# Hybrid stick-breaking and sparse attention: value products in one burst a unit later, low-part score pairs first and together

## The chip, the cores and the metric

One core of one Trainium2 chip. The metric is the device time of one launch in microseconds (us); lower is better. TensorE is called PE, VectorE DVE, ScalarE ACT, GpSimd POOL and SyncE SP; PEld is TensorE's weight load.

## The reference

Two decoder layers on 512 tokens of width 1024. In each layer two token mixers run on the same normalised input `h`, and their gated outputs are merged:

```python
proj = h @ w_in                      # 1024 x 5912, split into all the parts below
# (A) stick-breaking attention, 8 heads of 64, causal
z = q @ k.T * scale
w = where(mask, exp(log_sigmoid(z) + between), 0)   # between: reversed cumulative sum of log_sigmoid(-z)
o_a = w @ v
# (B) native sparse attention, 8 query heads, 2 key heads of 64
p_cmp = softmax(q @ kc.T)            # 31 compressed blocks
o_s = softmax(q @ k_slc.T) @ v_slc   # selected blocks: all 8 of 8, so causal attention
o_w = softmax(q @ k_win.T) @ v_win   # window of 512: causal attention too
o_b = g0 * o_cmp + g1 * o_s + g2 * o_w
merged = sigmoid(ga) * ((o_a * silu(z_a)) @ w_up_a) + sigmoid(gb) * ((o_b * silu(z_b)) @ w_up_b)
x = x + merged @ w_out
```

## The kernel before

Everything is float32. A product that must be exact is made from two halves: `hi` holds the operand rounded to the format that PE streams fast, `lo` the rest, and three products (hi by hi, hi by lo, lo by hi) are added up in one PSUM bank. PSUM's eight banks have fixed roles: `acc` (2), `S` (4, scores), `o` (1, output of the value products), `tp` (1, transposes and small things).

A layer has three stages.

- **X**: stick-breaking attention, 16 steps (four pairs of heads by four key blocks, `sb_qk`, `sb_cs`, `sb_pv`), with the projections for both attentions put between the steps.
- **Y**: sparse attention in 16 units, four query groups `j` by four query blocks `i`; unit `(j, i)` has `i + 1` key blocks. `nsa_qk` makes the scores of the two key heads for the selected and the window branch, takes the row maximum (DVE), the exponentials (ACT) and scales the rows by gate over sum (DVE) into `pr`. `nsa_pv` transposes `pr` by PE through `tp`, one key block (four 128x128 transposes) at a time, has ACT (even blocks) or DVE (odd blocks) copy the bank to `pT`, and multiplies by the values into `o` (four products for a key block in the source, eight instructions in the trace, two passes each). Between all this stand the products of the gate projections. `cmp_qk`, `cmp_t` and `cmp_pv` do the compressed branch once for each `j`.
- **Out**: the last three gate projections, the two up-projections and the output projection.

PE's order is written out by hand. A `Pacer` keeps a clock of its own (`mm` and `tr` add an estimate for each product), and `pump(us)` takes products from a queue of projections (`fill`) until that clock has moved on by so much. `Y_FILL` holds 21 projections of 24 products for stage Y; when they are used up, `pump` returns at once. In unit `u` stage Y pumps until `Y_LAT` (8 to 10 us) after the scores of that unit, emits the scores of unit `u + 1`, and then the transposes and value products of unit `u`. The other engines' orders come from a scheduler.

PE is used in three shapes. Most products and the transposes use the full 128 by 128 array. The value products have 64 output columns; those of the two key heads use the two column halves, side by side. The low-part score products have 64 contracted rows (`sK2` in stage X, `kN2` in stage Y); those of two heads use the two row halves, side by side, into two banks. The value products of both attentions are called column-split here, the low-part score pairs row-split.

Of the kernel before, what the change touches and what calls it, by code (L numbers as in the profile page):

```python
# [13 lines left out]
F32 = mybir.dt.float32  # L14
# [3 lines left out]
AF = mybir.ActivationFunctionType  # L18
# [4 lines left out]
P = 128  # L23
# [27 lines left out]
def kernel(  # L51
# [238 lines left out]

    def new_h():
        hs = H()
        hs.hh, hs.hl = [], []
        hs.ssq = cp.tile([P, S], F32, tag="ssq", name="ssq")
        return hs
# [46 lines left out]
    def mm(out, lhsT, rhs, start, stop, us, **kw):  # L342
        T.matmul(out, lhsT, rhs, start=start, stop=stop, **kw)  # L343
        pc.tick(us)
# [176 lines left out]
    def g_tile(tag, dt=F32, n=S):  # L521
        return gp.tile([P, n], dt, tag=tag, name=tag, bufs=dict(G_TAGS)[tag])
# [110 lines left out]
    for l in range(depth):  # L633
        yt = [None] * 4
        last = l == depth - 1
        with ExitStack() as lc:
# [111 lines left out]
            def mlp_w2(ht, hv2):  # L748
                with tc.high_priority(offset=PRIO_SB):
# [3 lines left out]
                    for t in range(2):  # L753
                        mm(pt[:, HD:P], hv2[:, t].rearrange("p a c -> p (a c)"), w2t[:, 1, t], False, t == 1, 0.2,
                           skip_group_check=True)
# [121 lines left out]
            def sb_qk(t):  # L877
# [5 lines left out]
                for h, z in enumerate(zb):  # L883
                    mm(z[:, :n], R.sK1[:, h, ks], R.sX[:, h, kb * P:], True, False, n * .00043)
                for h, z in enumerate(zb):
                    gs = slice(h * HD, (h + 1) * HD)
                    mm(z[:, :n], R.sK2[gs, ks], R.sX[gs, h, kb * P:], False, True, n * .00043)
                with tc.high_priority(offset=PRIO_SB):
# [105 lines left out]
            def nsa_qk(j, i):  # L994
# [10 lines left out]
                for hf, (a, b) in enumerate(halves):  # L1005
                    w = (b - a) * 256
                    for g in range(2):
                        mm(sb[g][hf][:, :w], nX[:, g, qs], kN1[g][:, a:b].rearrange("p k t c -> p (k t c)"),
                           True, False, w * .00043)
                    for g in range(2):  # L1010
                        gs = slice(g * HD, (g + 1) * HD)
                        mm(sb[g][hf][:, :w], nX[gs, g, qs], kN2[gs, a:b].rearrange("p k t c -> p (k t c)"),
                           False, b < nk, w * .00043)
                for g in range(2):
# [20 lines left out]

            def nsa_pv(o, pr, i, gap):
                nk = i + 1
                qs = slice(i * P, (i + 1) * P)
                pend = None

                def pv(kb, pT):
                    for t in range(2):
                        for g in range(2):
                            mm(o[g * HD:(g + 1) * HD, qs], vN[:, kb, t * P + g * HD:t * P + (g + 1) * HD],
                               pT[:, g, t], False, kb == nk - 1 and t == 1, 0.115, skip_group_check=True)

                for kb in range(nk):
                    pt = t_bank()
                    ptv = pt.rearrange("p (g t q) -> p g t q", g=2, t=2)
                    for g in range(2):  # L1050
                        for t in range(2):
                            tr(ptv[:, g, t], pr[g][:, kb, t], identf)
                    pT = py.tile([P, 2, 2, P], F32, tag="pT", name="pT", bufs=3)
                    with tc.high_priority(offset=PRIO_SB):
                        if kb % 2 == 0:
                            A.activation(pT.rearrange("p g t q -> p (g t q)"), pt, AF.Copy)  # L1056
                        else:
                            V.tensor_copy(pT.rearrange("p g t q -> p (g t q)"), pt)
                    if pend is not None:
                        pv(*pend)  # L1060
                    pend = (kb, pT)
                    pc.pump(gap)
                pv(*pend)

# [86 lines left out]
            with ExitStack() as ly:  # L1151
# [4 lines left out]
                ready = pc.now + Y_LAT[0]  # L1156
                for u in range(16):
                    j, i = u // NT, u % NT
                    pc.pump(ready - pc.now)
                    if u == 0:  # L1160
                        pcT = cmp_t(sc)
                    if u < 15:
# [4 lines left out]
                        if i == 2 and j < 2:  # L1167
                            set_nX(j + 2, n_q[j + 2])
                    if i == 0:
                        o = cmp_pv(pcT)  # L1170
                    nsa_pv(o, pr.pop(u), i, Y_GAP)
                    if i == 2 and j < 3:
                        pc.until(lambda: j + 1 in n_in)
                        sc = cmp_qk(j + 1)
                    if i == 3:
                        if ("z", j) in done:
                            V.scalar_tensor_tensor(yt[j][:, 1], o, 0.5, yt[j][:, 1], op0=ALU.mult, op1=ALU.mult)
                        else:
                            A.activation(yt[j][:, 1], o, AF.Copy)
                        done.add(("o", j))  # L1180
                        if j < 3:
                            pcT = cmp_t(sc)
                pc.drain()

        eng.copy = A.copy
        with ExitStack() as lc:
# [44 lines left out]
            if not last:  # L1231
                hs2 = new_h()
            for n in range(KD):
# [59 lines left out]
```

## Time and profile before

| | us |
|---|---|
| three timed runs | 1053.28, 1056.89, 1058.15 |
| their median | 1056.89 |
| the profiled execution: span on the core | 1055.7 |
| PE busy | 1015.3 (96%) |
| DVE busy | 754.2 (71%) |
| ACT busy | 443.2 (42%) |
| POOL busy | 253.8 (24%) |

The profile gives a span for its execution, from the first to the last instruction, and no time around it; the span lies between the timed runs, 1.2 us under their median. The chain of work that ended last is PE by 66%, DVE by 14%. Since matmuls are pipelined, what one costs is read from the distance of its start to the next one's start, not from its own duration. In the first layer stage X runs to about 224 us, stage Y to 426 us and the rest to 546 us; in the second layer the same stages end at about 738 us, 941 us and the end.

### The profile page before, as it was taken

Reading aid. Unit: us, or ns where it says so; the run is one execution under the profiler, and the core shown is the slowest. Engines: PE = TensorE matmul, PEld = TensorE weight load, DVE = VectorE, ACT = ScalarE, POOL = GpSimd, SP = SyncE. Lnnn points to the kernel's source line nnn. Section 1 sums busy time; section 2 is a strip of 40 time slices with the busy share of each in tenths; the row PEclk is TensorE's granted clock in tenths of the full one; section 3 lists DMA queues with packets and bytes.
Section 4 is the critical chain, followed back from the end, with each engine's and each line's share of the span. In section 5 each row is a group of like instructions: output and inputs, shape, how many; then the busy total and the mean of one; then the engine's idle time right before and its main releaser. Section 6 shows DMA issues by size and latency. Waiting matters only on the chain.

```text
span 1055.7 us, 14761 instructions
## 1 busy us (share of the span) xinstructions
PE 1015.3 (96%) x5379; PEld 775.3 (73%) x5379; DVE 754.2 (71%) x1468; ACT 443.2 (42%) x1070; POOL 253.8 (24%) x288
## 2 busy tenths in 40 slices
PE   7999899899999999999999989989999999999998
PEld 5876666677777777888887657757777777778886
DVE  7889878968777766575576987787886866665641
ACT  4453446654333332633333534565443323336221
POOL 4173454541111101000014525636201110100000
PEclk9999999999999999999999989989999999999999
DMA  8422334312221222244632223350312221224331
GB/s 280 118 61 61 85 100 109 76 41 65 56 61 41 61 61 60 80 122 121 177 105 71 65 69 99 85 124 20 80 49 53 60 61 40 62 60 140 96 107 57
DMA packets 161769, 88.05 MB, mean 83 GB/s; under 512 B 38417, under 2 KB 157473, under 8 KB 161697
## 3 DMA queue, kind: packets, MB, share of 16 engines
q1 hardware_dynamic: 160816, 84.99, 29.9%
q0 software_dynamic: 704, 2.11, 0.5%
q8 instruction: 42, 0.69, 0.3%
q14 instruction: 31, 0.25, 0.1%
q10 hardware_dynamic: 176, 0.03, 0.0%
HBM read 80.81 MB, written 6.29 MB: 83 GB/s over the span
## 4 chain that ended last, share of the span: by engine, by line
PE 66%; DVE 14%; issue 9%; POOL 6%; ACT 4%; DMA 2%; POOLq 0%; SPq 0%; ACTq 0%; DVEq 0%
PE acc L343 40%; PE S L343 14%; PE o L343 6%; PE tp L347 4%; DVE wlo L402 2%; POOL whi L160 1%; DVE f_t L683 1%; ACT y L490 1%; PE tp L343 1%; POOL sum L931 1%; ACT e L217 1%; DVE y L493 1%; DVE e L896 1%; POOL sum L930 1%; DMA raw<-in_w_in_dram 1%
## 5 line engine op out<-in xcount | busy, mean ns | idle before, releaser
L343 PE MATMUL acc<-hl,whi 128*128 128x512 f32 x640 | 259.7, 406 | 1.6 <-DVE hl L586 1.4
L343 PE MATMUL acc<-hh,whi 128*128 128x512 f32 x640 | 259.9, 406 | 1.0 <-DVE q L805 0.5
L160 POOL TENSOR_SCALAR whi<-raw 128x1024 fp32r<-128x1024 f32 (+1 forms) x84 | 100.0, 1192 | 510.1 <-PE acc L343 401.6
L343 PE MATMUL acc<-hh,wlo 128*128 128x512 f32 x640 | 181.9, 407 | 0.0
L402 DVE TENSOR_TENSOR wlo<-raw,whi 128x1024 fp32r<-128x1024 f32 (+1 forms) x124 | 158.4, 1277 | 13.9 <-POOL whi L160 7.9
L343 PEld LDWEIGHTS acc<-hl,whi 128*128 128x128 f32 x640 | 121.8, 190 | 33.8 <-issue 6.9
L343 PEld LDWEIGHTS acc<-hh,whi 128*128 128x128 f32 x640 | 122.0, 191 | 32.0 <-issue 4.3
L343 PEld LDWEIGHTS acc<-hh,wlo 128*128 128x128 f32 x640 | 118.0, 190 | 30.3 <-issue 7.5
L1025 ACT ACTIVATE pr<-S,mx 128x256 f32<-128x256 f32 (+1 forms) x192 | 81.4, 444 | 23.2 <-DVE mx L1022 11.7
L402 ACT CAST whi<-raw 128x1024 fp32r<-128x1024 f32 x40 | 42.0, 1050 | 116.2 <-PE S L343 42.4
L1056 ACT ACTIVATE pT<-tp 128x512 f32<-128x512 f32 x48 | 28.8, 599 | 147.4 <-PE tp L347 147.3
L1020 DVE TENSOR_REDUCE mx<-S 128x2 f32<-128x512 f32 (+1 forms) x96 | 53.1, 594 | 23.8 <-PE S L343 23.4
L217 ACT ACTIVATE e<-S 128x128 f32<-128x128 f32 (+3 forms) x64 | 25.3, 430 | 81.0 <-DVE S L892 76.8
L343 PE MATMUL acc<-whi,hh 128*128 128x256 f32 (+1 forms) x192 | 58.3, 304 | 0.3 <-ACT vN L661 0.3
L343 PE MATMUL acc<-wlo,hh 128*128 128x256 f32 (+1 forms) x192 | 54.9, 286 | 0.0
L343 PE MATMUL acc<-whi,hl 128*128 128x256 f32 (+1 forms) x192 | 54.9, 286 | 0.0
L1033 DVE TENSOR_SCALAR pr<-pr,rc 128x128 f32<-128x128 f32 (+3 forms) x128 | 53.4, 454 | 1.7
L343 PE MATMUL o<-pT,vN 128*64 128x128 f32 x640 | 52.6, 285 | 0.9 <-ACT pT L1056 0.9
L343 PE MATMUL S<-yh,wlo 128*128 128x512 f32 x128 | 50.8, 397 | 0.0
L343 PE MATMUL S<-yh,whi 128*128 128x512 f32 x128 | 50.7, 396 | 0.0
L343 PE MATMUL S<-yl,whi 128*128 128x512 f32 x128 | 50.1, 392 | 0.0
L343 PEld LDWEIGHTS o<-pT,vN 128*64 128x64 f32 x640 | 33.3, 136 | 20.7 <-issue 15.3
(316 smaller groups left out, 1902.4 us busy)
## 6 DMA issues: line engine op xcount, KB each, us to landing
raw<-in_w_in_dram SPq DMA_DIRECT2D x72, 512.0 KB, 3.8
raw<-in_w_in_dram SPq DMA_DIRECT2D x36, 256.0 KB, 3.7
raw<-in_cmp_w_dram SPq DMA_DIRECT2D x16, 512.0 KB, 4.6
raw<-in_w_out_dram SPq DMA_DIRECT2D x16, 512.0 KB, 4.0
raw<-in_w_up_a_dram SPq DMA_DIRECT2D x16, 256.0 KB, 3.0
raw<-in_w_up_b_dram SPq DMA_DIRECT2D x32, 128.0 KB, 3.3
gv<-xs SPq DMA_DIRECT2D x16, 256.0 KB, 2.7
x_sb<-in_x_dram SPq DMA_DIRECT2D x4, 512.0 KB, 6.6
```

Source lines behind the costliest of these rows:

```text
L160: G.tensor_scalar(dst, src, 1.0, 0.0, op0=ALU.mult, op1=ALU.add)
L217: ins = A.activation(dst, src, func, **kw)
L343: T.matmul(out, lhsT, rhs, start=start, stop=stop, **kw)
L347: T.transpose(out, in_, ident)
L402: for ins in (eng.copy(hi, rv), V.tensor_sub(lo, rv, hi.bitcast(F32))):
L490: copy(rot[a:a + 32], xq[b:b + 32])
L493: V.tensor_add(rot, xq, rot)
L683: V.tensor_tensor(f_v[hf][t * HD:(t + 1) * HD, :, a, g, 0:NCMP], src[:, :, t, hf:hf + NCMP], pe_v[:, hf * 8:(hf + 1) * 8, t:t + 1].to_broa ...
L1020: V.tensor_reduce(mx[:, hf, g], sbk[-1], axis=AX.XY, op=ALU.max, negate=True)
L1025: exps.append(A.activation(pr[g][:, a:b, t], sbk[hf][:, t], AF.Exp, bias=mx[:, 0, g, t:t + 1], accum_out=dn[:, hf, g, t:t + 1]))
L1033: V.tensor_scalar(pr[g][:, :nk, t], pr[g][:, :nk, t], rc[:, g, t:t + 1], None, op0=ALU.mult)
L1056: A.activation(pT.rearrange("p g t q -> p (g t q)"), pt, AF.Copy)
```

## The change

- In stage X `sb_qk` emits the two row-split low-part products ahead of the two full ones, so that they follow the column-split value products of step `t - 2`.
- In stage Y `nsa_qk` emits all low-part pairs of a unit first (of both halves of its keys), then all full products, then the mask products.
- `nsa_pv` is cut in two: `nsa_t` makes the transposes and copies of unit `u` with fill between them as before, and the value products of unit `u` stand in one burst, without fill, after the next pump and right ahead of the scores of unit `u + 2`. `pT` gets four buffers instead of three.
- The transposes of the compressed branch (`cmp_t`) move from the end of the unit before to just ahead of unit `i == 0`'s own transposes; `cmp_pv` moves behind these.
- The pacer counts a low-part product at half of what it counted.
- The square sums of the second layer take a `gx` buffer instead of one of their own, which is where the fourth `pT` finds room. One start flag in `mlp_w2` is set.

```diff
@@ sb_qk
                 for h, z in enumerate(zb):
-                    mm(z[:, :n], R.sK1[:, h, ks], R.sX[:, h, kb * P:], True, False, n * .00043)
+                    gs = slice(h * HD, (h + 1) * HD)
+                    mm(z[:, :n], R.sK2[gs, ks], R.sX[gs, h, kb * P:], True, False, n * .00022)
                 for h, z in enumerate(zb):
-                    gs = slice(h * HD, (h + 1) * HD)
-                    mm(z[:, :n], R.sK2[gs, ks], R.sX[gs, h, kb * P:], False, True, n * .00043)
+                    mm(z[:, :n], R.sK1[:, h, ks], R.sX[:, h, kb * P:], False, True, n * .00043)
...
@@ nsa_qk
                     for g in range(2):
-                        mm(sb[g][hf][:, :w], nX[:, g, qs], kN1[g][:, a:b].rearrange("p k t c -> p (k t c)"),
-                           True, False, w * .00043)
-                    for g in range(2):
                         gs = slice(g * HD, (g + 1) * HD)
                         mm(sb[g][hf][:, :w], nX[gs, g, qs], kN2[gs, a:b].rearrange("p k t c -> p (k t c)"),
+                           True, False, w * .00022)
+                for hf, (a, b) in enumerate(halves):
+                    w = (b - a) * 256
+                    for g in range(2):
+                        mm(sb[g][hf][:, :w], nX[:, g, qs], kN1[g][:, a:b].rearrange("p k t c -> p (k t c)"),
                            False, b < nk, w * .00043)
...
+            def nsa_t(pr, i, gap):
+                pTs = []
+                for kb in range(i + 1):
                     pt = t_bank()
...
-                    pT = py.tile([P, 2, 2, P], F32, tag="pT", name="pT", bufs=3)
+                    pT = py.tile([P, 2, 2, P], F32, tag="pT", name="pT", bufs=NT)
...
-                    if pend is not None:
-                        pv(*pend)
-                    pend = (kb, pT)
+                    pTs.append(pT)
                     pc.pump(gap)
-                pv(*pend)
+                return pTs
+
+            def nsa_pv(o, pTs, i):
+                qs = slice(i * P, (i + 1) * P)
+                for kb, pT in enumerate(pTs):
+                    for t in range(2):
+                        for g in range(2):
+                            mm(o[g * HD:(g + 1) * HD, qs], vN[:, kb, t * P + g * HD:t * P + (g + 1) * HD],
+                               pT[:, g, t], False, kb == i and t == 1, 0.115, skip_group_check=True)
...
@@ stage Y
-                for u in range(16):
+                o, pTs = None, None
+                for u in range(17):
                     j, i = u // NT, u % NT
                     pc.pump(ready - pc.now)
-                    if u == 0:
-                        pcT = cmp_t(sc)
+                    if u > 0:
+                        nsa_pv(o, pTs, (u - 1) % NT)
+                        if i == 0:
+                            nsa_o(j - 1, o)
+                    if u == 16:
+                        break
...
                     if i == 0:
+                        pcT = cmp_t(sc)
+                    pTs = nsa_t(pr.pop(u), i, Y_GAP)
+                    if i == 0:
                         o = cmp_pv(pcT)
-                    nsa_pv(o, pr.pop(u), i, Y_GAP)
```

What it moves, at the three places that the prediction speaks of. A row is one PE instruction of the source with its output, its operands and its size (xN: N equal ones that follow each other).

Stage X of the first layer, PE, a step with one key block (`sK1` is the full operand, `sK2` the low part). Before:

```order
L343 MATMUL o_702<-w_893,gv_191 64x384
L343 MATMUL S_925<-sX_677,sK1_678 128x128
L343 MATMUL S_926<-sX_677,sK1_678 128x128
L343 MATMUL S_925<-sX_677,sK2_679 128x128
L343 MATMUL S_926<-sX_677,sK2_679 128x128
L343 MATMUL acc_875<-hh_324,wlo_683 128x512
```

With the change:

```order
L342 MATMUL o_701<-w_892,gv_190 64x384
L342 MATMUL S_924<-sX_676,sK2_678 128x128
L342 MATMUL S_925<-sX_676,sK2_678 128x128
L342 MATMUL S_924<-sX_676,sK1_677 128x128
L342 MATMUL S_925<-sX_676,sK1_677 128x128
L342 MATMUL acc_874<-hh_323,wlo_682 128x512
```

The low-part pair now stands directly behind the value product, and the full products follow it.

Stage Y of the first layer, PE, from the last value product of group `j = 0` to the first transposes of group 1 (`kN_178`, `kN_179` are the full keys of the two heads before, `kN_180` the low part; 177, 178 and 179 with the change; `sc` belongs to the compressed branch, `mk_n` is the mask). Before:

```order
L343 MATMUL acc<-hl,whi 128x512
L343 MATMUL o<-pT,vN 64x128 x4
L347 MATMUL tp<-identf,sc 128x128 x2
L343 MATMUL S<-kN_178,nX 128x512
L343 MATMUL S<-kN_179,nX 128x512
L343 MATMUL S<-kN_180,nX 128x512 x2
L343 LDWEIGHTS identb
L343 MATMUL S<-mk_n,identb 128x256
L343 LDWEIGHTS identb
L343 MATMUL S<-mk_n,identb 128x256
L343 MATMUL o<-pcT,vcz 128x128 x4
L347 MATMUL tp<-identf,pr 128x128 x4
```

With the change:

```order
L342 MATMUL acc<-hl,whi 128x512
L342 MATMUL o<-pT,vN 64x128 x16
L342 MATMUL S<-kN_179,nX 128x512 x2
L342 MATMUL S<-kN_177,nX 128x512
L342 MATMUL S<-kN_178,nX 128x512
L342 LDWEIGHTS identb
L342 MATMUL S<-mk_n,identb 128x256
L342 LDWEIGHTS identb
L342 MATMUL S<-mk_n,identb 128x256
L346 MATMUL tp<-identf,sc 128x128 x2
L346 MATMUL tp<-identf,pr 128x128 x4
```

All value products of a unit stand in one burst, the low-part pair follows it, and both sets of transposes, which share the one bank `tp`, follow each other.

The end of stage Y in the first layer, PE, from the scores of the last unit on (the second layer's is the same). Before, it ends with:

```order
L347 MATMUL tp<-identf,pr 128x128 x4
L343 MATMUL o<-pT,vN 64x128 x4
L343 MATMUL acc<-hh,wlo 128x512 x3
L343 MATMUL o<-pT,vN 64x128 x4
L343 MATMUL acc<-hh,whi 128x512
```

With the change, from the mask product of the last unit's scores:

```order
L342 MATMUL S<-mk_n,identb 128x256
L346 MATMUL tp<-identf,pr 128x128 x4
L342 MATMUL acc<-hh,wlo 128x512 x5
L346 MATMUL tp<-identf,pr 128x128 x8
L342 MATMUL o<-pT,vN 64x128 x12
L346 MATMUL tp<-identf,pr 128x128 x16
L342 MATMUL o<-pT,vN 64x128 x16
L342 MATMUL acc<-hh,whi 128x512
```

The burst counts on the pacer's clock outside the pumped time, so the fill is used up earlier: after the last scores five fill products are left, where there were 58 before. The products behind the last row belong to the gate projections of the out stage; they stand behind the last value product before as after.

## Rows read from the trace of the kernel before

**Rows 1.** The page, busy time by engine: busy us (share of the span) xinstructions.

```profile
PE 1015.3 (96%) x5379; PEld 775.3 (73%) x5379; DVE 754.2 (71%) x1468; ACT 443.2 (42%) x1070; POOL 253.8 (24%) x288
```

**Rows 2.** Busy time in stretches, stage Y of each layer: stretch and length, then engines.

```profile
core 0: us, PE busy (x) PEld busy (x) DVE busy (x) ACT busy (x) POOL busy (x), PEclk, DMA share, GB/s
246.00:546.00 300.00, 300.00 (x1608) 231.11 (x1607) 198.40 (x386) 112.78 (x287) 27.28 (x29) 1.00 0.31 85
```

**Rows 3.** Timeline of PE, stage Y, value products: start us, duration us, instruction.

```profile
332.35 0.39 PE L343 MATMUL acc<-hh,whi 128*128 128x512 f32 x1
332.58 0.40 PE L343 MATMUL acc<-hl,whi 128*128 128x512 f32 x1
332.91 0.66 PE L343 MATMUL o<-pT,vN 128*64 128x128 f32 x8
333.50 0.44 PE L347 MATMUL tp<-identf,sc 128*128 128x128 f32 x2
...
359.84 0.33 PE L343 MATMUL o<-pT,vN 128*64 128x128 f32 x2
```

**Rows 4.** Timeline of PE, stage Y, scores of a unit with four key blocks.

```profile
354.94 2.15 PE L343 MATMUL S<-kN,nX 128*128 128x512 f32 x8
357.03 0.39 PE L343 MATMUL S<-mk_n,identb 128*128 128x256 bf16 x2
```

**Rows 5.** Timeline of PE, stage X, a value product, its step's scores and the fill after.

```profile
62.98 0.65 PE L343 MATMUL o<-w,gv 128*64 128x256 f32 x4
63.57 1.16 PE L343 MATMUL S<-sX,sK 128*128 128x512 f32 x4
64.66 0.50 PE L343 MATMUL acc<-hh,whi 128*128 128x512 f32 x1
64.99 0.39 PE L343 MATMUL acc<-hl,whi 128*128 128x512 f32 x1
```

**Rows 6.** Timeline of PE, stage X, row-split pair followed by a column-split product.

```profile
137.91 0.82 PE L343 MATMUL S<-sX,sK 128*128 128x256 f32 x4
138.65 1.52 PE L343 MATMUL acc<-raw,f_t 128*64 128x256 f32 x12
```

**Rows 7.** Timeline of PE's weight load after a value-product group.

```profile
331.09 0.19 PEld L343 LDWEIGHTS acc<-hl,whi 128*128 128x128 f32 x1 [0.17 <-issue]
```

**Rows 8.** Waits of PE over the whole span: total us, times, longest.

```profile
PE acc L343 <- DVE f_t L683: 6.9, 2, 3.5
PE tp L347 <- DVE mlp_u L733: 6.8, 2, 3.4
```

**Rows 9.** Timeline of PE and ACT, the compressed branch's transposes and their copy.

```profile
286.03 0.44 PE L347 MATMUL tp<-identf,sc 128*128 128x128 f32 x2
...
286.50 0.38 ACT L981 ACTIVATE pcT<-tp 128x256 f32<-128x256 f32 x1 [5.55 <-PE tp L347]
```

**Rows 10.** Timeline of PE, first transposes after the last scores of the first layer.

```profile
404.61 0.60 PE L347 MATMUL tp<-identf,pr 128*128 128x128 f32 x4
```

**Rows 11.** Timeline of DVE, then ACT, the last unit's softmax in the first layer.

```profile
403.39 2.60 DVE L1020 TENSOR_REDUCE mx<-S 128x2 f32<-128x512 f32 x4 [1.88 <-PE S L343]
...
407.31 0.69 DVE L1058 COPY pT<-tp 128x512 f32<-128x512 f32 x1 [0.42 <-PE tp L347]
...
412.40 0.88 DVE L1033 TENSOR_SCALAR pr<-pr,rc 128x512 f32<-128x512 f32 x2
...
405.31 0.60 ACT L1056 ACTIVATE pT<-tp 128x512 f32<-128x512 f32 x1 [7.65 <-PE tp L347]
406.85 0.47 ACT L1025 ACTIVATE pr<-S,mx 128x256 f32<-128x256 f32 x1 [0.95 <-DVE mx L1022]
...
410.36 0.24 ACT L1025 ACTIVATION_READ_ACCUMULATOR pr<-S,mx 128x1 f32 x1
```

**Rows 12.** Busy time in stretches around PE's wait for `mlp_u`, first layer (columns as in rows 2).

```profile
186.50:189.90 3.40, 0.45 (x2) 0.01 (x1) 3.34 (x7) 1.79 (x5) 0.56 (x1) 1.00 0.74 160
189.90:193.30 3.40, 2.96 (x8) 2.47 (x9) 2.73 (x9) 2.34 (x6) 1.88 (x5) 0.50 0.00 0
```

More of the change, by code (lines that the diff above doesn't have):

```diff
@@ L289, in x_block, with new_h @@
         split_x(hs, l, k, xk)
-    def new_h():
+    def new_h(ssq=None):
         hs = H()
-        hs.hh, hs.hl = [], []
-        hs.ssq = cp.tile([P, S], F32, tag="ssq", name="ssq")
+        hs.hh, hs.hl, hs.ssq = [], [], ssq
         return hs
@@ L753, in mlp_w2 @@
                     for t in range(2):
-                        mm(pt[:, HD:P], hv2[:, t].rearrange("p a c -> p (a c)"), w2t[:, 1, t], False, t == 1, 0.2,
+                        mm(pt[:, HD:P], hv2[:, t].rearrange("p a c -> p (a c)"), w2t[:, 1, t], t == 0, t == 1, 0.2,
                            skip_group_check=True)
@@ L1034, in nsa_qk @@
                 return pr
[L1036 to L1047, printed above, removed]
+            def nsa_t(pr, i, gap):
+                pTs = []
+                for kb in range(i + 1):
                     pt = t_bank()
@@ L1058, in nsa_pv, with nsa_o @@
                             V.tensor_copy(pT.rearrange("p g t q -> p (g t q)"), pt)
-                    if pend is not None:
-                        pv(*pend)
-                    pend = (kb, pT)
+                    pTs.append(pT)
                     pc.pump(gap)
-                pv(*pend)
+                return pTs
[6 more added lines that the diff above has]
+                               pT[:, g, t], False, kb == i and t == 1, 0.115, skip_group_check=True)
+            def nsa_o(j, o):
+                if ("z", j) in done:
+                    V.scalar_tensor_tensor(yt[j][:, 1], o, 0.5, yt[j][:, 1], op0=ALU.mult, op1=ALU.mult)
+                else:
+                    A.activation(yt[j][:, 1], o, AF.Copy)
+                done.add(("o", j))
             fills = {"sq": proj_sbq, "sk": proj_sbk, "vs": prep_vs, "cmp": lambda a: prep_cmp(), "k": prep_k,
@@ L1174 @@
                         sc = cmp_qk(j + 1)
[L1175 to L1182, printed above, removed]
                 pc.drain()
@@ L1231 @@
             if not last:
-                hs2 = new_h()
+                hs2 = new_h(g_tile("gx"))
             for n in range(KD):
```

## The prediction

> **What bounds the kernel now.** I read the page's busy times first: PE is busy for 1015.3 of 1055.7 us, DVE for 754.2 [rows 1]. Then the busy times by stretch: from 246 to 546 us, stage Y and the out stage of the first layer, PE is busy for 300.00 of 300.00 us at full clock, DVE for 198.40 [rows 2]. In that stretch the view of waits has no wait of PE. So in stage Y each tenth that PE saves goes into the time, as long as PE still finds work. In stage X it waits for chains of DVE and ACT (`f_t` 6.9 us, `mlp_u` 6.8 us in the two layers) [rows 8], so a saving there can turn into a longer wait. Last I read PE's timeline around the shapes that the change moves. The reader is to compare distances of starts there.
>
> **What a change of shape costs.** A fill product follows the one before it after 0.23 us (332.35 to 332.58). The step from a full product into value products takes 0.33 (332.58 to 332.91): 0.10 us of waiting. Eight value instructions, side by side in four pairs, take 0.59 until the transposes start (332.91 to 333.50). A pair is worth 0.11, from the durations of eight and of two: (0.66 - 0.33) / 3. Four are 0.44, so 0.15 more are lost, in the way out and in the first weights [rows 3]. The first full product after a split one takes 0.33 instead of 0.23 (64.66 to 64.99), 0.10 more [rows 5]. So a value burst between full products costs 0.10 + 0.15 + 0.10 = 0.35 us, whatever its length.
>
> For the low-part pairs: a step of stage X takes 1.09 us for two full products and one pair side by side (63.57 to 64.66), where three times 0.23 would be 0.69. The 0.40 that are over [rows 5] are 0.10 for the first full product behind the value products, 0.10 to wait for the shape, 0.10 for its weights and 0.10 to leave it. The next full product loses 0.10 again, so a pair by itself costs 0.40. In stage Y two halves of keys take 2.09 (354.94 to 357.03) where six products would take 1.38: 0.71, or 0.35 a pair, since the bf16 mask product behind loses little [rows 4].
>
> A pair directly behind a burst: I take 0.10 into the value shape, 0.05 for its first weights, 0.10 between the shapes, 0.10 for the pair's weights, 0.10 out and 0.10 for the first full product, 0.55 in all, where the two apart are 0.75. Only the opposite direction is in the trace: two full products and a pair, followed by `f_t` products in the column shape, take 0.74 where three times 0.12 would be 0.36, so 0.38 are over, as by way of a full product [rows 6]. So a direct step costs one step.
>
> The durations alone don't tell whether half of this is the weights. The load behind a value group starts at 331.09, not ahead of it [rows 7]. [...]
>
> **Stage Y, saved.** Before, both layers hold 80 value bursts (40 key blocks each) and 48 pair bursts (16 units with one half of keys, 16 with two): 80 x 0.35 less 0.01 where transposes follow = 27.2, 16 x 0.71 = 11.4, 16 x 0.35 = 5.6, together 44.2 us. After, there are 32 bursts and 32 pair groups; 28 pairs stand directly behind a burst: 28 x 0.55 + 4 x 0.35 + 4 x 0.40 = 18.4. Saved: **25.8 us**. Its cover is full: PE has no wait there before [rows 2].
>
> **Stage X, saved.** 28 pairs come to stand behind value products and save 0.20 each, 5.6 us. Eight `f_t` groups that followed a pair now follow a full product, and lose about 0.15 each, 1.2 us. Of the 4.4 left, some ends in front of DVE's and ACT's chains, which start no earlier [rows 8]: bounds 0 and 4, I take **2 us**.
>
> **The compressed branch, added.** `cmp_t` now stands right ahead of the unit's own transposes, and both use the one `tp` bank. Before, its two transposes start at 286.03 and ACT's copy of them runs from 286.50 to 286.88 [rows 9]; other work lies behind them. Now the next transposes wait for that copy: 0.85 less 0.22 for the two themselves, 0.63 us, eight times: 5 us. If ACT or DVE is busy with another unit's softmax at that moment it is more (up to 1 us each, 8 in all); if `sc` is copied at once and PE's queue had a wait anyway, it is 2. I take **+5 us**. Behind these transposes on PE stand fill products, which wait with them.
>
> **The end of stage Y, added.** The fill is used up with five products left after the last scores, where 58 were left. T0 is the start of the first transposes behind them, 404.61 [rows 10]. From there PE has five fill products (1.2 us), and then only what is bound to other engines. The second block's copy by DVE can only follow the four maxima, which end at 405.99; DVE's copy came at 407.31 and took 0.69 [rows 11]: T0 + 3.4. Then come the third transposes and the burst of unit 14 (12 pairs at 0.11 and the 0.35), until about T0 + 5.1. The last unit's softmax is due only at T0 + 8.7 before (412.40 + 0.88 = 413.28). It is a chain: maxima, eight exponentials on ACT from 406.85 to 410.60, and the scaling [rows 11]. With the change ACT also has the third block's copy (0.60, as the copy at 405.31) in front of it, and DVE the evacuations of the last fill: about T0 + 9.65. Then four blocks of transposes go through the one bank in turn, each cycle a transposition (0.60) and a copy (0.60 or 0.69), 1.3 us: three cycles, the last transposes, and the burst of 16 pairs (2.0): T0 + 15.7. PE's own work in it is 7.8 us, so it idles for 8 us in each layer. Bounds: 5, if the softmax is ready as early as before and copies overlap the burst; 11, if ACT's and DVE's queues put the copies behind other work. I take 8, in both layers: **+16 us**. The fill that was there before isn't lost, it was done earlier; what is lost is its use as a cover.
>
> [...]
>
> **At nothing.** The half price of a low-part product on the pacer moves fill, but PE's sum stays; it is in the end of stage Y. The fourth `pT` removes a wait for a buffer and costs nothing. The square sums in `gx` and the start flag: `gx` has been read long before the out stage, and a flag takes no time. The pairs ahead of the full products end the scores at the same moment.
>
> **The sum**, against the profiled execution: 1055.7 - 25.8 - 2 + 5 + 16 + 6 = 1054.9 us. The profiled span lies 1.2 us under the median of the timed runs, and half of that is added: **1055.5 us**. About 0.5% (5.3 us) is what a measurement of this kernel can tell from no change.
>
> **The rivals.**
>
> 1. Faster: the end of stage Y is cheaper. PE idles for only 5 us a layer, and short transposes in between keep the clock at 1.00; stage X passes on all 4 us and `cmp_t` costs 3: 1055.7 - 25.8 - 4 + 3 + 10 = 1039, with 2 us of clock a layer 1043. For it: while the fill is gone, DVE and ACT have less other work in front of the last softmax than they had before, and T0 + 8.7 may shrink instead of grow. Against it: the order of PE leaves nothing to run there.
> 2. Slower: the last softmax and its four cycles through the one bank stand uncovered. Idle 11 us, clock 5 us a layer, `cmp_t` 8: 1055.7 - 25.8 - 2 + 8 + 22 + 10 = 1068, and 1070 without stage X's gain. It decides from the point where the end of stage Y and its clock cost 14.5 us a layer: 1055.7 - 25.8 - 2 + 5 + 29 = 1062. For it: the chain from maxima to scaling is 10 us long, and PE has 5 us for it. Against it: copies and burst overlap.
> 3. The change doesn't do what it says: weights are loaded ahead anyhow, or a direct step between the two split shapes costs as much as two. Then only the waiting of 0.10 at each switch that is gone is saved. 128 bursts and pair groups, each entered and left, are 256 switches in stage Y before; 64 with 28 direct steps are 100 after. 156 x 0.10 = 15.6 us, and the sum is 1055.7 - 15.6 - 2 + 5 + 16 + 6 = 1065. For it: no direct step from the column to the row shape is in the trace. Against it: the 0.33 behind every split shape [rows 5], and the way back, which costs one step [rows 6]. [...]
>
> **How the numbers follow.** The forecast, all terms near the values taken, 0.44: that is within 5.3 us of the median. Rival 1: 0.33, since the saving is the best measured term and the losses are the ones that I can only bound. Rival 2: 0.17. Rival 3: 0.06, slower too. So faster 0.33, same 0.44, slower 0.23. The range goes from 1042, just under rival 1's 1043, to 1068, rival 2's first sum; the rest of both is left out. The likeliest case's own range is 1050 to 1061.
>
> **What would show it.** In the profile after: switches cost the same, so PE's busy time per layer in stage Y falls by some 13 us; value bursts take 0.11 a pair plus one entry; behind `sc`'s transposes PE waits about 0.6 us for ACT's `pcT` copy; PE's waits list `pr` and `pT` with some 8 us a layer at the end of stage Y, and the granted clock falls to 0.5 just behind. I am wrong on the end of stage Y if PE idles there for under 5 or over 11 us, on the clock if it stays at 1.00, and on the shapes if a pair straight behind a burst costs 0.2 us more or less than 0.55 for both.

## The result and the profile after

| | before | with the change |
|---|---|---|
| median of four runs, us | 1055.88 | 1064.05 |
| lowest and highest | 1053.28, 1058.15 | 1063.62, 1065.91 |
| span of the profiled execution | 1055.7 | 1061.9 |
| PE busy | 1015.3 | 995.7 |

The ratio is 1.0085 with a 95% interval of 1.0064 to 1.0105. The change made the kernel slower by 0.85%, where 1055.5 and no change that can be told was forecast. PE does the same work in 19.6 us less of busy time, and the time is longer all the same: the saving is there, and more than all of it came back as waiting.

Where PE waits, over the whole span of the changed kernel (total us, times, longest):

```profile
PE acc L342 <- DVE f_t L682: 12.3, 2, 6.2
PE tp L346 <- DVE pr L1034: 6.9, 4, 2.3
PE tp L346 <- DVE mlp_u L732: 6.6, 2, 3.3
PE o L342 <- ACT w L217: 5.5, 6, 1.6
PE tp L346 <- DVE pT L1050: 4.4, 6, 0.9
PE acc L342 <- DVE xq L468: 4.0, 3, 1.7
...
PE tp L346 <- ACT pcT L980: 3.8, 8, 0.5
...
PE tp L346 <- ACT pT L1048: 2.7, 4, 0.7
```

Against [rows 8]: `mlp_u` is as it was. New are `pr` and `pT` (14.0 us together, of which 13.0 lie at the end of stage Y, 6.5 in each layer) and `pcT` (3.8, the shared bank), all three forecast. Also new, and not forecast: `f_t` rose from 6.9 to 12.3 us. That wait is in stage X.

The shapes do what was worked out. PE's timeline in the changed kernel, a burst of one key block, the scores of the next unit behind it, and the mask product:

```profile
347.77 0.66 PE L342 MATMUL o<-pT,vN 128*64 128x128 f32 x8
348.36 1.52 PE L342 MATMUL S<-kN,nX 64*128 64x512 f32 x8
349.72 0.39 PE L342 MATMUL S<-mk_n,identb 128*128 128x256 bf16 x2
```

From 347.77 to 349.72 it takes 1.95 us. The work in it is four value pairs (0.44) and, over two halves of 512 and 256 columns, three times 0.23 and 0.12, in all 1.49: 0.46 over, and 0.10 of entry ahead of 347.77, is 0.56 for a burst and a pair together. Forecast was 0.55.

PE's timeline and that of its weight load, a fill product in a stream, then the burst and the pair:

```profile
346.08 0.40 PE L342 MATMUL acc<-hl,whi 128*128 128x512 f32 x1
...
345.85 0.19 PEld L342 LDWEIGHTS acc<-hl,whi 128*128 128x128 f32 x1
...
347.77 0.42 PEld L342 LDWEIGHTS o<-pT,vN 128*64 128x64 f32 x8 [0.35 <-issue]
348.36 0.30 PEld L342 LDWEIGHTS S<-kN,nX 64*128 64x128 f32 x4 [0.17 <-issue]
```

In the stream a load starts 0.23 us ahead of its product (345.85, 346.08). The first load of the burst and that of the pair start together with their first products (347.77, 348.36), so at a change of shape no weights are loaded ahead here.

The end of stage Y came much as it was worked out, too. PE's timeline from the first transposes behind the last scores (T0 = 410.30):

```profile
410.30 0.60 PE L346 MATMUL tp<-identf,pr 128*128 128x128 f32 x4
...
413.45 0.66 PE L346 MATMUL tp<-identf,pr 128*128 128x128 f32 x4 [0.94 <-DVE pT L1050]
414.04 1.53 PE L342 MATMUL o<-pT,vN 128*64 128x128 f32 x24
417.88 0.70 PE L346 MATMUL tp<-identf,pr 128*128 128x128 f32 x2 [2.31 <-DVE pr L1034]
419.71 0.84 PE L346 MATMUL tp<-identf,pr 128*128 128x128 f32 x2 [1.13 <-DVE pr L1034]
421.23 1.11 PE L346 MATMUL tp<-identf,pr 128*128 128x128 f32 x4 [0.69 <-ACT pT L1048]
423.13 1.11 PE L346 MATMUL tp<-identf,pr 128*128 128x128 f32 x4 [0.79 <-DVE pT L1050]
424.93 1.11 PE L346 MATMUL tp<-identf,pr 128*128 128x128 f32 x4 [0.69 <-ACT pT L1048]
425.98 3.54 PE L342 MATMUL o<-pT,vN 128*64 128x128 f32 x32
429.44 0.50 PE L342 MATMUL acc<-hh,whi 128*128 128x512 f32 x1
```

DVE, the last scaling of the softmax in the same stretch:

```profile
419.07 0.88 DVE L1034 TENSOR_SCALAR pr<-pr,rc 128x512 f32<-128x512 f32 x2
```

The softmax is ready at 419.95, T0 + 9.65. A cycle of transposes and copy takes 1.9 us (421.23 to 423.13), since the clock has fallen (four transposes take 1.11 us there, 0.60 at 410.30), and the fill goes on at T0 + 19.1. Busy time in stretches of that place (PE, PEld, DVE, ACT, POOL, then the granted clock):

```profile
416.00:418.00 2.00, 0.12 (x1) 0.14 (x1) 1.24 (x5) 2.00 (x11) 0.00 (x0) 1.00 0.79 232
418.00:420.00 2.00, 0.78 (x3) 0.32 (x2) 1.50 (x6) 0.45 (x2) 0.00 (x0) 0.75 0.01 3
420.00:422.00 2.00, 1.31 (x6) 0.90 (x5) 0.00 (x0) 0.60 (x1) 0.00 (x0) 0.50 0.00 0
```

After the 2 us in which PE is busy for 0.12, the granted clock is 0.75 over the next 2 us and 0.50 over the 2 us behind them.

The longer wait for `f_t` begins on two other engines. DVE, then POOL, in stage X of the first layer, changed kernel:

```profile
108.40 2.09 DVE L899 TENSOR_TENSOR sp<-e,sp 128x384 fp32r<-128x384 f32 x2
110.41 5.83 DVE L682 TENSOR_TENSOR f_t<-ct,pe_t 64x248 f32<-64x248 f32 x8
...
108.29 1.78 POOL L929 TENSOR_TENSOR sum<-sp 128x256 f32<-128x256 f32 x2 [3.59 <-DVE sp L898]
110.03 1.93 POOL L930 TENSOR_TENSOR sum<-sp 128x256 f32<-128x256 f32 x2
111.93 1.84 POOL L931 TENSOR_TENSOR sum<-sum 128x256 f32<-128x256 f32 x2
```

The same two lines of DVE, and what POOL does next, before the change:

```profile
109.04 1.02 DVE L900 TENSOR_TENSOR sp<-e,sp 128x384 fp32r<-128x384 f32 x2
109.97 4.19 DVE L683 TENSOR_TENSOR f_t<-ct,pe_t 64x248 f32<-64x248 f32 x8
...
119.54 1.16 POOL L160 TENSOR_SCALAR whi<-raw 128x1024 fp32r<-128x1024 f32 x1 [13.82 <-PE S L343]
120.66 2.05 POOL L930 TENSOR_TENSOR sum<-sp 128x256 f32<-128x256 f32 x2
```

Before, POOL's order has a weight conversion ahead of these sums. It waits until 119.54, and the sums behind it, so POOL stands still while DVE makes `f_t`. After, the scheduler has put the sums ahead of the conversion; they run beside DVE's additions, and both of DVE's groups take longer, by 1.07 and 1.64 us. That makes the 2.7 us by which PE waits longer for `f_t` in each layer. That is the theory for stage X; for stage Y the theory is the prediction's own sum.

### The profile page after: what moved, and what is told of

Same layout as the page of the kernel before. It is cut to its first block, busy times and chain, and to the rows that moved or that the text cites. A ratio compares the mean times of both kernels' runs of the same rounds, so it can differ in the third digit from the quotient of the medians.

```text
span 1061.9 us, 14784 instructions
## 1 busy us (share of the span) xinstructions
PE 995.7 (94%) x5379; PEld 778.9 (73%) x5379; DVE 750.9 (71%) x1468; ACT 443.5 (42%) x1070; POOL 247.2 (23%) x288
## 4 chain that ended last, share of the span: by engine, by line
PE 67%; DVE 14%; issue 8%; ACT 6%; POOL 4%; DMA 1%; POOLq 0%; SPq 0%; DVEq 0%; ACTq 0%
PE acc L342 42%; PE S L342 15%; PE o L342 5%; PE tp L346 4%; DVE wlo L401 1%; DVE f_t L682 1%; ACT pr L1026 1%; ACT e L217 1%; POOL whi L160 1%; PE tp L342 1%; DVE e L895 1%; DVE kN L697 1%; ACT e L893 1%; DVE yy L482 1%; DVE xq L484 1%
## 5 line engine op out<-in xcount | busy, mean ns | idle before, releaser
L160 POOL TENSOR_SCALAR whi<-raw 128x1024 fp32r<-128x1024 f32 (+1 forms) x84 | 95.4, 1136 | 444.8 <-PE acc L342 393.2
L342 PE MATMUL acc<-hh,wlo 128*128 128x512 f32 x640 | 179.0, 402 | 0.0
L1026 ACT ACTIVATE pr<-S,mx 128x256 f32<-128x256 f32 (+1 forms) x192 | 81.6, 446 | 31.4 <-DVE mx L1023 15.7
L401 ACT CAST whi<-raw 128x1024 fp32r<-128x1024 f32 x40 | 42.0, 1050 | 122.0 <-PE S L342 42.4
L346 PE MATMUL tp<-identf,pr 128*128 128x128 f32 x320 | 53.8, 290 | 18.0 <-DVE pr L1034 6.9
L346 PEld LDWEIGHTS tp<-identf,pr 128*128 128x128 f32 x320 | 39.1, 147 | 31.9 <-DVE pT L1050 8.2
L1034 DVE TENSOR_SCALAR pr<-pr,rc 128x128 f32<-128x128 f32 (+3 forms) x128 | 48.7, 423 | 1.6
```

The lines of the kernel that those rows point to most:

```text
L160: G.tensor_scalar(dst, src, 1.0, 0.0, op0=ALU.mult, op1=ALU.add)
L346: T.transpose(out, in_, ident)
L401: for ins in (eng.copy(hi, rv), V.tensor_sub(lo, rv, hi.bitcast(F32))):
L1026: exps.append(A.activation(pr[g][:, a:b, t], sbk[hf][:, t], AF.Exp, bias=mx[:, 0, g, t:t + 1], accum_out=dn[:, hf, g, t:t + 1]))
L1034: V.tensor_scalar(pr[g][:, :nk, t], pr[g][:, :nk, t], rc[:, g, t:t + 1], None, op0=ALU.mult)
```

## The experiments

Each run's ratio is to the kernel before, run beside it on the same chip, with its 95% interval. A difference in us between two runs is one of medians; the kernel before had medians from 1054.28 to 1055.88 us beside the runs, so such a difference is good to 1 or 2 us. PE's idle time is the span less its busy time. "Low-part first" stands for the edit of the order of products, "price" for what the pacer counts for a low-part product.

**Stage X undone.** Full products first and the old price in `sb_qk`; the rest is the changed kernel.

```diff
-                    mm(z[:, :n], R.sK2[gs, ks], R.sX[gs, h, kb * P:], True, False, n * .00022)
+                    mm(z[:, :n], R.sK1[:, h, ks], R.sX[:, h, kb * P:], True, False, n * .00043)
...
-                    mm(z[:, :n], R.sK1[:, h, ks], R.sX[:, h, kb * P:], False, True, n * .00043)
+                    mm(z[:, :n], R.sK2[gs, ks], R.sX[gs, h, kb * P:], False, True, n * .00043)
```

> Stage X as before (full products first, low-part products at their old price on the pacer), stage Y and all else as changed. Theory: stage X lost 3.9 us and the step from X to Y 1.6 us by the change, so the time falls from 1064 by 3 to 6 us, to 1058 to 1061, and the two waits for f_t are back at 3.5 us each. Rival (the loss is all in stage Y): it stays within 1063 to 1066.

Measured: 1055.23 us, 1.0008 (0.9993 to 1.0022). `f_t` is back at 6.9 us in two waits. The edit in stage X cost 8.8 us, more than the 3 to 6 that were expected. Stage Y's whole change, as it stands, is worth nothing within 2.3 us: savings and losses cancel, as the sum had it.

**The old price alone.** Low-part products first in stage X, as in the change, at the price of before.

```diff
-                    mm(z[:, :n], R.sK2[gs, ks], R.sX[gs, h, kb * P:], True, False, n * .00022)
+                    mm(z[:, :n], R.sK2[gs, ks], R.sX[gs, h, kb * P:], True, False, n * .00043)
```

> Changed kernel, low-part products of stage X first, but at their old price on the pacer. Theory (the price alone moved fill and POOL's sums against DVE's f_t work): the two waits for f_t are back at 3.5 us each, the pairs keep their saving of 3 us a layer, and the time is 1054 to 1058. Rival (the order of the products itself delays the softplus chain): waits as in the changed kernel, 6.2 us each, 1062 to 1066.

Measured: 1054.60 us, 0.9994 (0.9974 to 1.0013). One number on the pacer, which neither adds nor takes away an instruction, is worth 9.4 us (1064.05 to 1054.60). The order of POOL with it is that of before, a conversion ahead of those sums. POOL, then the waits of PE:

```profile
119.66 1.05 POOL L160 TENSOR_SCALAR whi<-raw 128x1024 fp32r<-128x1024 f32 x1 [15.25 <-DMA raw<-in_w_in_dram]
...
PE o L342 <- ACT w L217: 8.3, 10, 1.6
PE acc L342 <- DVE f_t L682: 6.9, 2, 3.5
```

The saving of the pairs in stage X passes on only in part: against the run before this one it is 0.6 us, which the intervals don't tell from nothing, while the waits for `w` are 2.4 us longer (8.3 here, 5.9 there).

**The pump shorter by the burst.** The changed kernel, with the burst counted inside the pumped time.

```diff
-                    pc.pump(ready - pc.now)
+                    pc.pump(ready - pc.now - (0.46 * ((u - 1) % NT + 1) if u > 0 else 0.0))
```

> Changed kernel, but the value burst counts inside the pumped time (the pump ahead of it is shorter by 0.46 us for each key block), so that fill lasts to the end of stage Y. Theory: 8.7 us of idle PE and 3.7 us of half clock at the end of Y vanish in each layer, and the time is 1038 to 1046. Rival (scores wait for a softmax that the shorter pump no longer covers, or the bursts cost as much as the old groups): over 1055.

Measured: 1044.37 us, 0.9886 (0.9856 to 0.9915), 19.7 us less than the changed kernel. The end of stage Y had cost about what the sum says (16 + 6). In the traces PE's idle time falls by 13.1 us (66.2 to 53.1) and its busy time by 5.9 (995.7 to 989.8).

**Both edits.** The last two together: the old price in stage X and the shorter pump.

> Both of the last two edits. Theory: the gains add up, 1030 to 1038, faster than the kernel before by 1.7 to 2.5%. Rival (they share the same slack): no better than the run with the pump edit alone.

Measured: 1033.33 us, 0.9789 (0.9765 to 0.9813): 2.1% faster than before, and 21.3 us less than with the old price alone. The end of stage Y in this kernel, by busy time (columns as above), and the waits of PE in all of stage Y of the first layer:

```profile
393.00:414.30 21.30, 21.30 (x150) 17.33 (x148) 12.18 (x25) 8.76 (x24) 2.10 (x2) 1.00 0.24 65
```

```profile
PE tp L346 <- ACT pcT L980: 1.9, 4, 0.5
...
PE tp L346 <- DVE pr L1034: 0.8, 1, 0.8
PE tp L346 <- DVE sc L971: 0.7, 1, 0.7
PE tp L346 <- DVE pT L1050: 0.6, 1, 0.6
```

From 393.00 to 414.30 PE is busy through, at full clock. The cover is back, and the bursts keep their saving.

**The price in the kernel before.** Full products first, nothing else of the change.

```diff
-                    mm(z[:, :n], R.sK2[gs, ks], R.sX[gs, h, kb * P:], False, True, n * .00043)
+                    mm(z[:, :n], R.sK2[gs, ks], R.sX[gs, h, kb * P:], False, True, n * .00022)
```

> Kernel before, with one edit: the low-part products of stage X count at half price on the pacer; no product changes its place within its step. Theory (the price alone moves the fill, and with it POOL's sums into DVE's f_t work): waits for f_t of 6 us each instead of 3.5, and 1059 to 1065. Rival (the price hurts only together with the new order of the products): 1052 to 1057.

Measured: 1058.89 us, 1.0035 (1.0021 to 1.0048), just under the theory's range and above the rival's. The wait for `f_t` is that of the changed kernel, and POOL's sums stand beside DVE's additions as there. The wait, then POOL:

```profile
PE acc L343 <- DVE f_t L683: 12.4, 2, 6.2
...
108.77 1.78 POOL L930 TENSOR_TENSOR sum<-sp 128x256 f32<-128x256 f32 x2 [3.21 <-DVE sp L899]
```

So the price lengthens this wait without the new order of products. It costs 3.4 us here and 9.4 in the changed kernel. In the traces PE's idle time grows by 4.1 us here (40.4 to 44.5) and its busy time stays (1015.3, 1014.7). In the changed kernel, against the run with the old price, the idle time grows by 5.8 (60.4 to 66.2) and the busy time too, by 2.8 (992.9 to 995.7), at a mean granted clock of 0.975 where it was 0.983.

**POOL's sums behind `f_t`.** The changed kernel with one wait more, in one step of each layer: `behind` makes the first of POOL's sums wait for `f_last[0]`, the last of the `f_t` additions.

```diff
-                    G.tensor_add(t1, h0.bitcast(F32), h1.bitcast(F32))
+                    first = G.tensor_add(t1, h0.bitcast(F32), h1.bitcast(F32))
+                    if R is sb_in[1] and kb == 1:
+                        behind(first, f_last[0])
```

> Changed kernel, with one added wait: POOL's sums of the step beside the second set of f_t additions start behind the last of these additions. The order on PE and DVE is that of the changed kernel. Theory (POOL's work at the same time slows DVE's): the eight f_t additions take 4.2 us instead of 5.8, the two waits for f_t fall from 6.2 to about 3.5 us each, and the time falls from 1064 to 1057 to 1060. Rival (DVE is late for its own order, POOL has no part in it): f_t additions stay at 5.8, and the time at 1063 to 1067.

Measured: 1058.12 us, 1.0017 (1.0000 to 1.0035), 5.9 us less than the changed kernel, although a wait was added. DVE and POOL at that place:

```profile
108.77 1.02 DVE L906 TENSOR_TENSOR sp<-e,sp 128x384 fp32r<-128x384 f32 x2
109.71 4.18 DVE L689 TENSOR_TENSOR f_t<-ct,pe_t 64x248 f32<-64x248 f32 x8
...
113.97 1.41 POOL L936 TENSOR_TENSOR sum<-sp 128x256 f32<-128x256 f32 x2 [8.90 <-DVE f_t L689]
```

Without POOL beside them DVE's groups take 1.02 and 4.18 us again, and POOL's own additions 1.41 instead of 1.78. So here the two engines hold each other up, DVE's additions with 5.83 against 4.18 us, but neither stands still for the whole of the other's work: alone the five groups take 1.02, 4.18 and three times 1.41 us, 9.43 in all, and beside each other, in the changed kernel, they are through in 7.95 (108.29 to 116.24).

Of the 9.4 us of the price some 5.9 go with this wait. The other 3.5 are not longer waits: PE idles for 59.9 us here, no more than with the old price (60.4), but is busy for 2.8 us more with the same products (995.7 against 992.9), at a mean granted clock of 0.978 against 0.983. From execution to execution of this one kernel the time goes with that clock, from 1053.52 us at 0.983 to 1060.19 at 0.975. So the rest is, as the author's estimate from these clocks, PE at a lower granted clock for longer; what lowers it is not shown.

**The compressed branch's transposes earlier**, on top of both edits.

```diff
+                    if i == 0 and u < 16:
+                        pcT = cmp_t(sc)
                     if u > 0:
                         nsa_pv(o, pTs, (u - 1) % NT)
...
-                    if i == 0:
-                        pcT = cmp_t(sc)
                     pTs = nsa_t(pr.pop(u), i, Y_GAP)
```

> The kernel with both edits (pump shorter by the burst, old price in stage X), and the transposes of the compressed branch moved ahead of the value burst and the scores, apart from the unit's own transposes. Theory: the eight waits for the copy of these transposes (3.8 us in all) vanish, 1028 to 1031. Rival (another bank or the burst takes their place): 1032 to 1035.

Measured: 1033.05 us, 0.9788 (0.9764 to 0.9811), no different. The rival's time held, and in part its reason: the waits for `pcT` are gone, and the wait for `sc` has grown from 1.4 us to 4.0.

```profile
PE tp L346 <- DVE sc L971: 4.0, 2, 2.0
```

At the start of stage Y the compressed scores are not scaled yet, once in each layer, 2.0 us. But over the whole span PE idles for 4.3 us less than with both edits (43.1, 47.4); it is busy for 4.7 us more (987.8, 983.1). Busy time around the wait for `sc` in the first layer (columns as above):

```profile
234.30:237.70 3.40, 1.38 (x8) 0.56 (x6) 3.25 (x14) 1.61 (x9) 1.05 (x1) 1.00 0.00 0
237.70:241.10 3.40, 3.40 (x11) 2.58 (x12) 2.91 (x4) 0.99 (x4) 0.00 (x0) 0.50 0.14 24
```

Behind the wait PE is granted 0.50; with both edits alone the second of these stretches has 1.00. The 4.3 us of idle time that were saved came back as 4.7 us of busy time.

**Stage Y's scores in the old order**, on top of both edits: in each half the full products, then the pair.

```diff
                     for g in range(2):
+                        mm(sb[g][hf][:, :w], nX[:, g, qs], kN1[g][:, a:b].rearrange("p k t c -> p (k t c)"),
+                           True, False, w * .00043)
+                    for g in range(2):
                         gs = slice(g * HD, (g + 1) * HD)
                         mm(sb[g][hf][:, :w], nX[gs, g, qs], kN2[gs, a:b].rearrange("p k t c -> p (k t c)"),
-                           True, False, w * .00022)
-                for hf, (a, b) in enumerate(halves):
-                    w = (b - a) * 256
-                    for g in range(2):
-                        mm(sb[g][hf][:, :w], nX[:, g, qs], kN1[g][:, a:b].rearrange("p k t c -> p (k t c)"),
-                           False, b < nk, w * .00043)
+                           False, b < nk, w * .00022)
```

> The kernel with both edits, but stage Y's scores in their old order: in each half the full products first, then the low-part pair. The bursts stay. Theory (a direct step from burst to pair saves 0.15 us in 16 units with one half and 0.51 us in 16 with two): 10 us slower than with the pairs first, 1041 to 1046. Rival (only 0.10 us of waiting at each switch is saved, weights are loaded ahead): 5 us slower, 1037 to 1040.

Measured: 1037.43 us, 0.9835 (0.9811 to 0.9859), 4.1 us slower than with the pairs first. By its time that is the rival, by its trace it is not. PE's timeline of the same unit, with the pairs first, then with the full products first:

```profile
289.12 0.66 PE L342 MATMUL o<-pT,vN 128*64 128x128 f32 x8
289.70 1.51 PE L342 MATMUL S<-kN,nX 64*128 64x512 f32 x8
291.05 0.39 PE L342 MATMUL S<-mk_n,identb 128*128 128x256 bf16 x2
```

```profile
290.38 0.66 PE L342 MATMUL o<-pT,vN 128*64 128x128 f32 x8
290.97 1.91 PE L342 MATMUL S<-kN,nX 128*128 128x512 f32 x8
292.82 0.39 PE L342 MATMUL S<-mk_n,identb 128*128 128x256 bf16 x2
```

1.93 us against 2.44: 0.51 saved, to the hundredth what was worked out. Averaged over the units with two halves of keys it is 0.48, over the twelve with one half behind a burst 0.09 instead of 0.15; 16 x 0.48 and 12 x 0.09 are 8.8 us. In the shorter units PE then meets waits that the slower ones did not have: `pr` 0.8 and `pT` 0.6 in the first layer (waits above), 2.7 us in both. Where the rest of the difference went is open.

**Full products first in stage X**, on top of both edits.

```diff
-                    mm(z[:, :n], R.sK2[gs, ks], R.sX[gs, h, kb * P:], True, False, n * .00043)
+                    mm(z[:, :n], R.sK1[:, h, ks], R.sX[:, h, kb * P:], True, False, n * .00043)
...
-                    mm(z[:, :n], R.sK1[:, h, ks], R.sX[:, h, kb * P:], False, True, n * .00043)
+                    mm(z[:, :n], R.sK2[gs, ks], R.sX[gs, h, kb * P:], False, True, n * .00043)
```

> The kernel with both edits (pump shorter by the burst, old price in stage X), but with the full products first in stage X, as before. Theory (28 pairs behind value products save 3 us of PE time a layer, and the waits for w and f_t take most of it back): 1033 to 1036, at most 2 us slower than with the pairs first. Rival (the saving passes on): 1037 to 1039.

Measured: 1036.52 us, 0.9825 (0.9803 to 0.9848), 3.2 us slower than with the pairs first, between the two theories. `w` and `f_t` are waited for about as long in both kernels (7.0 and 6.9 us here, 6.7 and 6.9 with the pairs first).

**The burst alone**, with the shorter pump, full products first in both stages: the edits of the last two runs together.

> The burst and the shorter pump alone: full products first in stage X and in stage Y, as before. Theory (the burst alone removes 48 of 80 value groups, 48 times 0.35 is 17 us): 1037 to 1041. Rival (most of the gain needs the pairs behind the burst): 1045 to 1052.

Measured: 1039.83 us, 0.9853 (0.9829 to 0.9877), as expected. The burst is worth 15 us by itself, each of the two orders of pairs some 3 more on top of it.

**The pump shorter by twice the burst**, on top of both edits.

```diff
-                    pc.pump(ready - pc.now - (0.46 * ((u - 1) % NT + 1) if u > 0 else 0.0))
+                    pc.pump(ready - pc.now - (0.92 * ((u - 1) % NT + 1) if u > 0 else 0.0))
```

> The kernel with both edits, but the pump ahead of a burst is shorter by 0.92 us for each key block instead of 0.46. Theory (the pump is also the cover of the next softmax; shorter than it was, PE waits for the exponentials and for pr inside stage Y): 1036 to 1046. Rival (there is room left, and more fill at the end is no loss): 1031 to 1035.

Measured: 1037.67 us, 0.9836 (0.9811 to 0.9858). The time is in the theory's range, its reason isn't seen: in stage Y of the first layer PE waits 1.2 us for `pr`, where it waited 0.8, and over the whole span it idles for 46.9 us, where it idled for 47.4. Its profile has a granted clock of 0.50 from 541.90 to 543.90 us instead, at the start of the second layer, where no edit was made; with both edits it is 1.00 from 414.70 to 556.00. Inconclusive as to the cause; a larger term gains nothing.

## Why the prediction was wrong

- **The shapes** (25.8 us): right. A burst and a pair cost 0.56 where 0.55 was forecast, and a unit with two halves saves 0.48 to 0.51 where 0.51 follows from the forecast; one with one half saves 0.09 instead of 0.15. What rival 3 rests on, weights loaded ahead across shapes, does not hold here: the loads start with their first products (347.77, 348.36). In the time, the edits of stage Y are worth 18.3 us with the cover in place (1054.8 to 1036.5, the kernel before against pairs first in stage Y alone). The 25.8 less the 3.8 of `pcT` and the 2.7 of `pr` and `pT` are 19.3, a microsecond more.
- **The end of stage Y and the clock** (16 + 6): right. The fill went on at T0 + 19.1; the forecast was 15.7 and 3 of clock (its own terms behind T0 + 9.65 add up to 16.2 rather than 15.7). PE waits 13.0 us there in both layers, forecast 16. No run shows the 6 us of clock as a term by itself; what the runs showed there is a granted clock of 0.50 (420 to 422 us), four transposes in 1.11 us instead of 0.60, and 5.9 us less of PE's busy time once the cover was back (third run, 995.7 to 989.8). Giving the cover back was worth 21.3 us (second and fourth run). That the softmax was ready at T0 + 9.65, as forecast, is luck to the hundredth: the exponentials start 4.40 us behind T0 (414.70), 2.24 before (406.85 less 404.61), and half of that was made up behind them.
- **The compressed branch** (+5): 3.8 by the waits. Right in kind; but taking these waits away gained nothing, since `sc` was late (waits of 4.0 us) and the granted clock fell to 0.50 behind that wait.
- **Stage X, order** (-2): between -0.6 and -3.2 by the runs, the first not told from nothing. Right within that.
- **"At nothing. The half price of a low-part product on the pacer moves fill, but PE's sum stays; it is in the end of stage Y."** This is the step that failed. It costs 9.4 us. PE's sum does stay; but the price also moved the moments at which the scheduler orders POOL's queue, and a POOL that had stood still beside DVE's `f_t` additions now works beside them. PE then waits 5.4 us longer for `f_t`; the rest is not told apart in full, but goes with a lower granted clock (0.978 against 0.983). With 9.4 instead of 0 the prediction's sum is 1055.5 + 9.4 = 1064.9, and 1064.05 was measured. That is closer than the single terms were met (5 against 3.8, 2 against 0.6 to 3.2), so it is partly luck.

The time lies inside the range, but outside the likeliest case's own 1050 to 1061. The change was slower, by 0.85%, and the rival that had that sign (the end of stage Y and its clock above 14.5 us a layer) is not the reason: that end cost 21.3 us in both layers, 10.7 in each, where the forecast took 11. Rival 3's time, 1065, is the nearest to the measured one, but by chance: bursts and pairs cost what the forecast had, not what that rival had. What the prediction could have seen is in the diff and in the order: the price is changed in stage X too, and POOL's instructions there come in another order. The prediction looks at PE's order alone, and at POOL by its busy time, 24%.

## What to carry to other kernels

A planner's estimate is an edit like any other: whoever changes what a step counts for changes the order on every queue, and should compare all of them, the idle engines' most of all. Work that is moved out of a timed stretch must be paid for in that stretch, or the filler runs out where the last chain stands uncovered: here one term in the pump, together with the old price, turned a change that was 0.85% slower into one that is 2.1% faster.

## What the runs showed of the hardware that was not expected

Additions on DVE and on POOL slowed each other, although `f_t` and POOL's sums have no data in common: eight DVE additions took 4.18 us alone and 5.83 beside POOL's, POOL's pair of additions 1.41 alone and 1.78 beside DVE's. Here an engine that waited in its queue was worth more than one that worked: before, a weight conversion that was held up until 119.54 kept POOL out of DVE's way, and in the changed kernel one wait more on POOL took 5.9 us off the time.

In one run a short wait of PE cost twice. With the compressed branch's transposes earlier PE waited 2.0 us for `sc` and was busy for 1.38 of 3.40 us around it; the next 3.40 us were granted 0.50, and a run that idled for 4.3 us less than with both edits alone was no faster (1033.05 against 1033.33 us).
